# Loading the first tile in two pieces: the largest absolute value of each row, 8192 x 8192

## The chip, the cores and the metric

The kernel runs on one core of a Trainium2 chip. The metric is device time in microseconds (us) of one execution, the median of several; smaller is better. The core has several engines with queues of their own; this kernel uses VectorE (DVE) for all arithmetic, SyncE (SP) to issue nearly all transfers, ScalarE (ACT) for one store and GpSimd (POOL) for a few memory fills and the closing work. Sixteen DMA engines move the data.

## The reference

```
def setup_inputs():
    rows = 8192
    cols = 8192
    return {"x": np.random.randn(rows, cols).astype(np.float32)}

def reference(x):
    return np.linalg.norm(x, ord=np.inf, axis=1)
```

Along axis 1 of a matrix this norm is the largest absolute value of each row: 8192 rows of 8192 numbers give 8192 numbers. All 268.4 MB are read once; 32 KB are written.

## The kernel before

A tile is 128 partitions by 16384 columns of float32: each partition holds two neighbouring rows (B = 2), 64 KB that also lie together in memory. Three tiles have room at once (BUFS = 3). The 8192 rows are 32 such tiles, in three groups.

The bulk is 24 tiles, loops over `a` (A = 6) and `n` (G = 4). Each is one load of 8.4 MB by SP (L303) and one reduce by DVE, through the helper `absmax` (its instruction stands at L296), which takes the maximum of absolute values along the columns of both rows and writes two numbers per partition into `r_bulk`. The reduce of a tile waits for its load; the load of a tile waits for the reduce that last read its buffer, three tiles back. The first three loads wait for no reduce.

The next seven tiles, listed in `TAIL`, come in two to five loads by columns each (L315), with a reduce for each piece of a row into `part`. The last tile, `LAST`, comes in twelve loads (L341), from 2176 columns down to 768, so that little work is left when the last byte lands. Then SP stores `r_tail` (L359); ACT has stored `r_bulk` a little earlier (L357).

Loads rotate over eight completion semaphores. Where a load's semaphore is still in use, SP waits for the load eight places ahead.

After the program has been built, five functions edit it. Two matter here. `start_first_load_early` takes the first transfer that SP issues in the body, which must wait for nothing, and puts it at the very start of SP's program, ahead of the opening meeting of the engines (a barrier in which they wait for one another before the body begins). Exactly one transfer is moved; SP's next ones follow the meeting. `finish_on_pool` puts the waits for the last transfers and the clearing of semaphores on POOL at the end; it finds the last store's semaphore by itself.

The lines that the change touches are the load in the bulk's loop:

```
t = sbuf.tile([P, W + PAD], F32, tag="t")
nc.sync.dma_start(out=t[:, :W], in_=x_b[a, n])
```

W is 16384; PAD is 256 spare columns that the last tile uses.

Of the kernel before, what the change touches and what calls it, by code (L numbers as in the profile page):

```python
# [33 lines left out]


HEAD, STEP = 32, 8


def segments(loads, cols):

    out, at = [], 0
    for i, w in enumerate(loads):
        end = at + w
        while at < end:
            r = at // cols
            to = min(end, (r + 1) * cols)
            out.append((i, r, at - r * cols, to - at))
            at = to
    return out
# [201 lines left out]
@with_exitstack  # L251
def kernel(
    ctx: ExitStack,
    tc: tile.TileContext,
    x: bass.AP,
    out: bass.AP,
    G: int = 4,
    B: int = 2,
    BUFS: int = 3,
    PAD: int = 256,  # L260
    LINE: int = 128,
):
    nc = tc.nc
    P = nc.NUM_PARTITIONS
    rows, cols = x.shape
    W = B * cols


    n_tail = B * (len(TAIL) + 1)
    n_bulk_rows = rows // P - n_tail  # L270
    assert n_bulk_rows % (G * B) == 0
    A = n_bulk_rows // (G * B)
    split = n_bulk_rows * P
    x_b = x[:split].rearrange("(a p n b) c -> a n p (b c)", p=P, a=A, n=G, b=B)
    out_b = out[:split].rearrange("(a p n b) -> p a (n b)", p=P, a=A, n=G, b=B)
    x_t = x[split:].rearrange("(p t b) c -> t p (b c)", p=P, b=B)
    out_t = out[split:].rearrange("(p t) -> p t", p=P)

    outp = ctx.enter_context(tc.tile_pool(name="outp", bufs=1))
    sbuf = ctx.enter_context(tc.tile_pool(name="sbuf", bufs=BUFS))  # L280

    segs = [segments(loads, cols) for loads in TAIL]
    k_max = max(sum(r == b for _, r, _, _ in s) for s in segs for b in range(B))
    parts_of = [sum(r == b for r, _ in LAST) - 1 for b in range(B)]
    assert sum(parts_of) <= PAD

    r_bulk = outp.tile([P, A, G * B], F32)
    r_tail = outp.tile([P, n_tail], F32)
    part = outp.tile([P, n_tail - B, k_max], F32)
    used = [HEAD, A * G * B, n_tail, (n_tail - B) * k_max]  # L290
    gap = -sum(-(-n // STEP) * STEP for n in used) % LINE
    outp.tile([P, gap], F32, name="gap")
    nc.gpsimd.memset(part[:], 0.0)  # L293

    def absmax(o, i):
        return nc.vector.reduce_max(  # L296
            out=o, in_=i, axis=X, apply_absolute_value=True
        )

    for a in range(A):  # L300
        for n in range(G):
            t = sbuf.tile([P, W + PAD], F32, tag="t")
            nc.sync.dma_start(out=t[:, :W], in_=x_b[a, n])  # L303
            absmax(
                r_bulk[:, a, n * B : (n + 1) * B],
                t[:, :W].rearrange("p (b c) -> p b c", b=B),
            )

    for i, loads in enumerate(TAIL):
        t = sbuf.tile([P, W + PAD], F32, tag="t")  # L310
        todo = segs[i]
        seen = [0] * B
        at = 0
        for j, w in enumerate(loads):
            nc.sync.dma_start(out=t[:, at : at + w], in_=x_t[i][:, at : at + w])  # L315
            at += w
            for _, b, c, n in [s for s in todo if s[0] == j]:
                k, lo = seen[b], b * cols + c
                absmax(part[:, i * B + b, k : k + 1], t[:, lo : lo + n])
                seen[b] += 1  # L320

    def after(ins, first, kind):
        info = mybir.DependencyInfo(kind, mybir.DependencyReason.SCHED_ONLY)
        tc.add_manual_dep(ins.ins, first.ins.name, info, reason="order")


    t = sbuf.tile([P, W + PAD], F32, tag="t")
    left = parts_of[:]
    col = [0] * B
    at, slot = 0, {}  # L330
    ends = [w for _, w in LAST[-B:]]
    lo = W - sum(ends)
    for b in range(B):
        slot[b] = -(-lo // LINE) * LINE + ends[b]
        lo = slot[b] + parts_of[b]
    assert lo <= W + PAD
    for j, (b, w) in enumerate(LAST):
        final = left[b] == 0
        to = slot[b] - w if final else at
        frm = b * cols + col[b]  # L340
        nc.sync.dma_start(out=t[:, to : to + w], in_=x_t[len(TAIL)][:, frm : frm + w])  # L341
        col[b] += w
        if final:
            r = n_tail - B + b
            absmax(r_tail[:, r : r + 1], t[:, to : slot[b] + parts_of[b]])
        else:
            left[b] -= 1
            k = slot[b] + left[b]
            done = absmax(t[:, k : k + 1], t[:, to : to + w])
            at += w  # L350
        if j == 0:

            ins = absmax(r_tail[:, : n_tail - B], part[:])
            after(ins, done, mybir.DependencyClass.NoSync)
        if j == len(LAST) - 4:

            ins = nc.scalar.dma_start(out=out_b, in_=r_bulk[:])  # L357
            after(ins, done, mybir.DependencyClass.Sync)
    nc.sync.dma_start(out=out_t, in_=r_tail[:])  # L359
    nc.at_finalize(clear_partials_early)  # L360
    nc.at_finalize(drop_implied_waits)
    nc.at_finalize(start_first_load_early)
    nc.at_finalize(finish_on_pool)
    nc.at_finalize(open_without_vector)
# [30 lines left out]
```

## Time and profile before

| what | value |
|---|---|
| time, median of 3 runs | 626.8 us (626.56 to 627.16) |
| time of the profiled execution | 626.44 us |
| its span, first to last instruction | 623.8 us |
| read from memory | 268.44 MB, 430 GB/s over the span |
| DVE | 63 instructions, 552.4 us busy |
| bulk reduces | 24, 17.22 us each |
| loads of bulk tiles | 24, median 40.7 us from issue to landing |

The profile is one execution, taken by the hardware profiler; durations below come from it. A load's time to landing contains the time that it queues behind earlier loads: with a tile's data taking about 19.4 us (the distance between two landings in the bulk), 40.7 us means that one whole tile was ahead of it. A transfer moves as packets; a packet here is one partition's contiguous piece, and each of the sixteen DMA engines carries the packets of eight partitions. The trace records every packet with its start, duration and size. "Idle before" is time in which an engine had nothing to run, with what ended it.

### The profile page before, as it was taken

Reading aid. Unit: us, or ns where it says so; the run is one execution under the profiler, and the core shown is the slowest. Engines: PE = TensorE matmul, PEld = TensorE weight load, DVE = VectorE, ACT = ScalarE, POOL = GpSimd, SP = SyncE. Lnnn points to the kernel's source line nnn. Section 1 sums busy time; section 2 is a strip of 40 time slices with the busy share of each in tenths; the row PEclk is TensorE's granted clock in tenths of the full one; section 3 lists DMA queues with packets and bytes.
Section 4 is the critical chain, followed back from the end, with each engine's and each line's share of the span. In section 5 each row is a group of like instructions: output and inputs, shape, how many; then the busy total and the mean of one; then the engine's idle time right before and its main releaser. Section 6 shows DMA issues by size and latency. Waiting matters only on the chain.

```text
span 623.8 us, 151 instructions
## 1 busy us (share of the span) xinstructions
DVE 552.4 (89%) x63; POOL 0.3 (0%) x5
## 2 busy tenths in 40 slices
DVE  0588988889988899888898888988889999999999
POOL 0000000000000000000000000000000000000000
DMA  9999999999999999999999999999999999999998
GB/s 403 471 403 454 420 433 441 403 471 403 471 403 462 412 454 420 437 437 403 471 403 471 403 471 403 454 420 450 424 434 406 432 448 422 431 435 432 426 426 350
DMA packets 8849, 268.47 MB, mean 430 GB/s; under 512 B 1680, under 2 KB 1680, under 8 KB 3088
## 3 DMA queue, kind: packets, MB, share of 16 engines
q1 hardware_dynamic: 8064, 268.44, 99.7%
q10 hardware_dynamic: 784, 0.02, 0.1%
q14 instruction: 1, 0.01, 0.0%
HBM read 268.44 MB, written 0.03 MB: 430 GB/s over the span
## 4 chain that ended last, share of the span: by engine, by line
DMA 63%; DVE 36%; another core or an unknown queue 0%; issue 0%
DMA t<-in_x_dram 63%; DVE r_bulk L296 25%; DVE part L296 8%; DVE t L296 3%; DVE r_tail L296 0%
## 5 line engine op out<-in xcount | busy, mean ns | idle before, releaser
L296 DVE TENSOR_REDUCE r_bulk<-t 128x2 f32<-128x16384 f32 x24 | 413.3, 17220 | 70.4 <-DMA t<-in_x_dram 70.4
L296 DVE TENSOR_REDUCE part<-t 128x1 f32<-128x8192 f32 (+19 forms) x26 | 121.3, 4737 | 0.3
L296 DVE TENSOR_REDUCE t<-t 128x1 f32<-128x1792 f32 (+7 forms) x10 | 16.3, 1689 | 0.0
L296 DVE TENSOR_REDUCE r_tail<-t 128x1 f32<-128x772 f32 (+1 forms) x2 | 1.8, 952 | 0.0
L296 DVE TENSOR_REDUCE r_tail<-part 128x14 f32<-128x42 f32 x1 | 0.2, 184 | 0.0
L293 POOL MEMSET part<- 128x42 f32 x1 | 0.1, 133 | 0.0
L379 POOL MEMSET const-bfloat16-1.0<- 128x1 bf16 x1 | 0.1, 101 | 0.0
L379 POOL MEMSET const-uint8-127<- 128x1 uint8 x1 | 0.1, 101 | 0.0
L379 POOL MEMSET const-float32-0.0<- 128x1 f32 x1 | 0.1, 98 | 0.2 <-issue 0.2
L379 POOL MEMSET const-float32-1.0<- 128x1 f32 x1 | 0.1, 98 | 0.0
## 6 DMA issues: line engine op xcount, KB each, us to landing
t<-in_x_dram SPq DMA_DIRECT2D x2, 4672.0 KB, 37.5
t<-in_x_dram SPq DMA_DIRECT2D x2, 3520.0 KB, 36.2
t<-in_x_dram SPq DMA_DIRECT2D x1, 6336.0 KB, 36.3
t<-in_x_dram SPq DMA_DIRECT2D x1, 5696.0 KB, 40.4
t<-in_x_dram SPq DMA_DIRECT2D x2, 1792.0 KB, 34.3
t<-in_x_dram SPq DMA_DIRECT2D x1, 3392.0 KB, 37.6
t<-in_x_dram SPq DMA_DIRECT2D x1, 3008.0 KB, 44.2
t<-in_x_dram SPq DMA_DIRECT2D x1, 2496.0 KB, 27.3
```

Of the source, the lines that this page charges most:

```text
L293: nc.gpsimd.memset(part[:], 0.0)
L296: return nc.vector.reduce_max(out=o, in_=i, axis=X, apply_absolute_value=True)
L379: nc = _bacc.Bacc("TRN2", target_bir_lowering=False, num_devices=1)
```

## The change

In the bulk's loop, the first tile's load (a = n = 0) is cut at column 1024: one load of columns 0 to 1023 (512 KB, 4,096 bytes a partition) and one of columns 1024 to 16383 (7.5 MB, 61,440 bytes a partition). All other tiles are loaded as before. The first reduce still reads the whole tile.

```
@@ -34,6 +34,9 @@
 HEAD, STEP = 32, 8
+
+
+FIRST = 1024
@@ -300,7 +303,9 @@
     for a in range(A):
         for n in range(G):
             t = sbuf.tile([P, W + PAD], F32, tag="t")
-            nc.sync.dma_start(out=t[:, :W], in_=x_b[a, n])
+            cuts = [0, FIRST, W] if a == n == 0 else [0, W]
+            for lo, hi in zip(cuts, cuts[1:]):
+                nc.sync.dma_start(out=t[:, lo:hi], in_=x_b[a, n][:, lo:hi])
             absmax(
                 r_bulk[:, a, n * B : (n + 1) * B],
                 t[:, :W].rearrange("p (b c) -> p b c", b=B),
```

In the built program SP now issues 58 transfers instead of 57. The one that `start_first_load_early` moves ahead of the opening meeting is the load of 1024 columns; the load of 15360 columns is SP's first after it. The first reduce waits for two semaphores. Every later load uses the next of the eight semaphores, and the lists of the other engines are otherwise the same.

More of the change, by code (lines that the diff above doesn't have):

```diff
@@ L36 @@
 HEAD, STEP = 32, 8
+FIRST = 1024
 def segments(loads, cols):
@@ L302 @@
             t = sbuf.tile([P, W + PAD], F32, tag="t")
-            nc.sync.dma_start(out=t[:, :W], in_=x_b[a, n])
+            cuts = [0, FIRST, W] if a == n == 0 else [0, W]
+            for lo, hi in zip(cuts, cuts[1:]):
+                nc.sync.dma_start(out=t[:, lo:hi], in_=x_b[a, n][:, lo:hi])
             absmax(
```

## The prediction

> **What bounds the kernel now.** I read the page first (who is busy, what the end hangs on), then the rates of three long stretches, the chain of waits, and last the first six microseconds, where the edit acts.
>
> ```profile
> DVE 552.4 (89%) x63; POOL 0.3 (0%) x5
> DMA  9999999999999999999999999999999999999998
> DMA 63%; DVE 36%; another core or an unknown queue 0%; issue 0%
> L296 DVE TENSOR_REDUCE r_bulk<-t 128x2 f32<-128x16384 f32 x24 | 413.3, 17220 | 70.4 <-DMA t<-in_x_dram 70.4
> ```
>
> The DMA engines are full in nearly every one of the 40 slices. VectorE (DVE) is 89% busy and its only real idle time, 70.4 us, is spent waiting for loads of bulk tiles.
>
> ```profile
> core 0: us, DVE busy (x) POOL busy (x), PEclk, DMA share, GB/s
> 8.00:466.00 458.00, 396.05 (x23) 0.00 (x0) 1.00 1.00 434
> 466.00:600.00 134.00, 133.33 (x26) 0.00 (x0) 1.00 1.00 429
> 600.00:620.00 20.00, 20.00 (x12) 0.00 (x0) 1.00 1.01 422
> ```
>
> The last column is the rate. It holds 434 GB/s through the whole bulk, and falls a little in the tail, where loads are narrower and packets shorter. So the stream of loads has no hole that a better order could fill.
>
> ```profile
> 0.73 0.07 issue
> 0.79 40.36 DMA t<-in_x_dram
> 41.16 0.02 issue
> 41.18 17.22 DVE r_bulk L296
> ...
> 466.41 17.22 DVE r_bulk L296
> 483.63 17.26 DVE part L296 x3
> ```
>
> The columns are start, duration, and what held the chain. It runs from the second load's issue at 0.79 through landings and reduces. From 466.41 to the end DVE never idles noticeably: the reduce that starts there waited for the last bulk tile, and all that follows is DVE work or loads of the tail. A stream that is late by some amount in its first microseconds therefore ends late by that amount; one that is early gains it.
>
> ```profile
> 0.00 0.36 SPq L303 DMA_DIRECT2D t<-in_x_dram  x1
> 0.79 0.33 SPq L303 DMA_DIRECT2D t<-in_x_dram  x1
> DMA  0000009999900000000000009990909000000000
> 21.88 17.22 DVE L296 TENSOR_REDUCE r_bulk<-t 128x2 f32<-128x16384 f32 x1 [21.88 <-DMA t<-in_x_dram]
> 41.18 17.22 DVE L296 TENSOR_REDUCE r_bulk<-t 128x2 f32<-128x16384 f32 x1 [2.08 <-DMA t<-in_x_dram]
> ```
>
> SP issues the first load at 0.00 and the second, behind the opening meeting of the engines, at 0.79. The third line covers 0 to 6 us in slices of 0.15 and marks where packets start: sixteen between 0.99 and 1.55, one for each DMA engine, and the next sixteen from 3.73 on. The packet records give the sizes: a full load is 128 packets of 65,536 bytes, eight for each engine. The first sixteen took 2.74 to 3.23 us, nearly all later ones 2.418. The difference, 0.32 to 0.81 us, is a start-up cost paid once.
>
> **The change, part by part.** The 8.4 MB load that SP issues ahead of everything becomes one of 0.52 MB (128 packets of 4,096 bytes); the rest (128 packets of 61,440 bytes) is issued behind the opening meeting, where the load of the second tile stood. No other instruction is added or removed.
>
> *Packets.* In the tail, a load 1024 columns wide exists: its 128 packets took 159 ns each. A packet of 61,440 bytes has no row; between the rows for 50,688 bytes (1,872 ns) and 65,536 (2,418), a straight line gives 1,872 + 546 x 10,752 / 14,848 = 2,267 ns. Together 2,426 against 2,418: 8 ns a partition, eight partitions an engine, 0.067 us. Its bounds are 0.03 (the 422 of the last stretch against 434, for 0.52 MB: 1.242 against 1.208 us) and 0.13 (twice the worked value). On the path, since the stream has no slack.
>
> *Completion.* One more load is one more four-byte packet on each engine, 9 ns in the records. On the path: 0.009 us.
>
> *The hole that may open.* Until now 19 us of data covered the 0.79 us to the second issue. Now 0.52 MB must. On one engine that data lasts, from its first packet, 0.32 of start-up plus 8 x 159 ns = 1.59 us. If issue to first packet takes the second load what it took the first (0.99 to 1.55, by engine; ScalarE's late store took 0.92, from 620.33 to 621.25), the second's packets are ready 0.79 us after the first's on the same engine. The margin is 1.59 - 0.79 = 0.80 us. I take zero, hidden by the first load's own data; without that cover each further microsecond costs one. The third issue before took 0.70 us instead of 0.33, as if the issue path were briefly full; were that 0.37 to fall on the second half, 0.43 of margin remains.
>
> *Start-up.* How short packets behave on sixteen cold engines no row shows. The lower bound: every engine pays only the smallest excess; the last starter would be at 1.55 + 2.42 + 0.32 = 4.29 where the slowest first packet now ends at 4.62, so -0.33 us. The upper: the largest excess is paid again by the long packets, +0.81. I take 0, because the first load still starts at the same point and meets the same 0.32 to 0.81.
>
> *Waits and queues.* The first reduce now waits for two loads. Late in the trace, a DVE semaphore wait in front of a reduce takes 0.07 us (622.00 to 622.08). Behind it queues the second reduce, which idles 2.08 us for its own load, so it is hidden; uncovered it would cost 0.07. SP issues each load one place later: the loads of the second and third tile leave SP some 0.4 and 0.7 us later, with about 19 and 38 us of data ahead of them. Uncovered, that would cost those amounts. Loads rotate over eight completion semaphores, so each later load changes semaphore, but a tail load that waits for the one eight places ahead still waits for the same data. ScalarE's store shifts likewise. Zero.
>
> The sum is 0.067 + 0.009, about +0.08 us. The profiled execution took 626.44 us, 623.8 of span and 2.64 around it, so 626.52. The median shown is 626.8, 0.36 above the profiled run; measured as that was, 626.9.
>
> **A rule that speaks against it.** The Trainium skill, page "DMA: Bandwidth & Descriptors", section "Anatomy of one DMA", fits about 2.0 us fixed per DMA plus bytes over 436 GB/s, for GpSimd's path; its "Rules for kernel authors" ask for at least 1 MiB a load. Charged in full, the extra load of half that size would make the sum 628.9. The trace disagrees for queued loads: the tail's loads of 0.4 to 1.1 MB run at 422 GB/s, so the fixed part overlaps with the neighbour. It would return if the queue ran dry between the two.
>
> **The rivals.** *The stream runs dry (slower).* The second half comes after the first has drained. For: only 0.80 us of cover, and one trace's opening. Against: the waits listed for the built program show none between the halves but the opening meeting. Price, with the second half held until the first has landed: landing follows the last packet by 0.33 us in the first tile, then 1.55 to the same last engine's packet, then another start-up of 0.32 to 0.81: 2.2 to 2.7 us, about 629.2. It shows beyond 0.2% when the second issue comes later than 0.79 + 0.80 + 1.25 = 2.84 us after the first. 18% for this or another loss above 1.25 us.
>
> *A better start (faster).* Short packets get all engines going at once. Evenly warm engines give -0.33 + 0.08, so 626.55, which is no measurable change; to exceed 0.2% nearly all of 0.99 + 0.81 = 1.80 us before full flow would have to vanish, for 625.0 at best. 12%, since the cold start is the one thing the trace can't show with short packets.
>
> *The gain that a smaller first piece suggests is hidden anyway.* Reducing while the rest arrives would need a reduce of the piece alone; here one reduce waits for both. Even an earlier first reduce would only lengthen DVE's idle time before the second, 2.08 us now. It gives 626.9 too and belongs to the forecast.
>
> **How the numbers follow.** Forecast, no change: 70%; runs dry or some other loss: 18%; better start: 12%. Within 0.2% (1.25 us, about what a measurement of this kernel can tell from no change) means 625.55 to 628.05; the unknown costs alone span 626.8 - 0.33 + 0.04 = 626.5 to 626.8 + 0.81 + 0.14 = 627.75. With part of either rival, the range is 625.6 to 628.6.
>
> **What would show it.** Right: second issue near 0.79; 4,096-byte packets of about 159 ns after the first; long packets following on each engine without a gap; first reduce within 21.5 to 22.8; 434 GB/s in the bulk. Wrong: a blank stretch after the first sixteen groups of short packets, short packets far above 159 ns, a first reduce beyond 23.1 (21.88 + 1.25) or before 20.6, or a bulk rate off 434, since 1% there is over 4 us.

## The result, and the profile after

The changed kernel takes 627.62 us (median of 21 runs, 626.56 to 629.06) against 626.64 us (21 runs, 626.43 to 627.35): a ratio of 1.0016, interval 1.001 to 1.0022. That is 0.98 us slower, inside the band of 0.2% that the forecast called no change, and yet more than its interval. The runs lie nearly three times as wide as before's (2.50 us against 0.92), so part of the loss differs from one execution to the next.

Two rows of the changed kernel's page, who is busy and the bulk reduces:

```profile
DVE 552.5 (88%) x63; POOL 0.3 (0%) x5
L299 DVE TENSOR_REDUCE r_bulk<-t 128x2 f32<-128x16384 f32 x24 | 413.3, 17220 | 71.2 <-DMA t<-in_x_dram 71.2
```

DVE's work is unchanged, and it waited 0.8 us longer for bulk tiles (71.2 against 70.4). The rate over the first of the three stretches:

```profile
8.00:466.00 458.00, 396.05 (x23) 0.00 (x0) 1.00 1.00 432
```

The bulk ran at 432 GB/s instead of 434. Now the reduces of the early tiles, changed kernel first, then before. The bracket holds DVE's idle time ahead of each reduce.

```profile
21.97 17.22 DVE L299 TENSOR_REDUCE r_bulk<-t 128x2 f32<-128x16384 f32 x1 [21.97 <-DMA t<-in_x_dram]
41.24 17.22 DVE L299 TENSOR_REDUCE r_bulk<-t 128x2 f32<-128x16384 f32 x1 [2.05 <-DMA t<-in_x_dram]
...
99.66 17.22 DVE L299 TENSOR_REDUCE r_bulk<-t 128x2 f32<-128x16384 f32 x1 [2.29 <-DMA t<-in_x_dram]
119.13 17.22 DVE L299 TENSOR_REDUCE r_bulk<-t 128x2 f32<-128x16384 f32 x1 [2.25 <-DMA t<-in_x_dram]
138.68 17.22 DVE L299 TENSOR_REDUCE r_bulk<-t 128x2 f32<-128x16384 f32 x1 [2.33 <-DMA t<-in_x_dram]
...
177.37 17.22 DVE L299 TENSOR_REDUCE r_bulk<-t 128x2 f32<-128x16384 f32 x1 [2.05 <-DMA t<-in_x_dram]
```

```profile
99.24 17.22 DVE L296 TENSOR_REDUCE r_bulk<-t 128x2 f32<-128x16384 f32 x1 [2.11 <-DMA t<-in_x_dram]
118.55 17.22 DVE L296 TENSOR_REDUCE r_bulk<-t 128x2 f32<-128x16384 f32 x1 [2.09 <-DMA t<-in_x_dram]
137.89 17.22 DVE L296 TENSOR_REDUCE r_bulk<-t 128x2 f32<-128x16384 f32 x1 [2.12 <-DMA t<-in_x_dram]
...
176.59 17.22 DVE L296 TENSOR_REDUCE r_bulk<-t 128x2 f32<-128x16384 f32 x1 [2.10 <-DMA t<-in_x_dram]
```

The first two tiles arrive almost as before (21.97 against 21.88, 41.24 against 41.18). Then each load comes a little too late: in the rows shown DVE idles 2.25 to 2.33 us where before it idles 2.09 to 2.12. At 177.37 it is over, the loss stands at 0.78 us and grows by 0.03 more to the last bulk reduce (467.22 against 466.41).

The rest was lost at the very end. The chain of waits, before:

```profile
607.52 13.51 DVE t L296 x9
621.03 0.18 issue
621.21 0.81 DVE r_tail L296
```

and of the changed kernel, with one row of its list of waits:

```profile
608.35 13.75 DVE t L299 x9
622.10 0.28 issue
622.37 0.47 DVE r_tail L299
```

```profile
DVE r_tail L299 <- DVE t L299: 0.3, 1, 0.3
```

Consecutive reduces overlap: each starts about 0.08 us before the one ahead ends. The second last one, the first into `r_tail`, did so before (621.21, with the reduce ahead ending at 621.29). Now it starts 0.29 us after that end, though the load that it waits for had landed at 621.86, half a microsecond before that start, and DVE had passed its wait for it at 621.89. So the profiled spans differ by 0.09 (first reduce) + 0.72 (bulk) + 0.36 (tail) - 0.01 = 1.16 us, which is 624.96 - 623.80.

### The profile page after: what moved, and what is told of

It is laid out like the page before. It is cut to its first block, busy times and chain, and to the rows that moved or that the text cites. A ratio compares the mean times of both kernels' runs of the same rounds, so it can differ in the third digit from the quotient of the medians.

```text
span 625.0 us, 153 instructions
## 1 busy us (share of the span) xinstructions
DVE 552.5 (88%) x63; POOL 0.3 (0%) x5
## 4 chain that ended last, share of the span: by engine, by line
DMA 63%; DVE 36%; another core or an unknown queue 0%; DVEq 0%; issue 0%; SPq 0%
DMA t<-in_x_dram 63%; DVE r_bulk L299 25%; DVE part L299 8%; DVE t L299 3%; DVEq L395 0%; DVE r_tail L299 0%; SPq L308 0%
## 5 line engine op out<-in xcount | busy, mean ns | idle before, releaser
L299 DVE TENSOR_REDUCE r_bulk<-t 128x2 f32<-128x16384 f32 x24 | 413.3, 17220 | 71.2 <-DMA t<-in_x_dram 71.2
```

The source lines that it names most:

```text
L299: return nc.vector.reduce_max(out=o, in_=i, axis=X, apply_absolute_value=True)
```

## The experiments

Theory A: the cut itself is cheap, but starting sixteen engines on short packets leaves them in a pattern in which they slow one another until it settles. Theory B: the loss is that of any cut. Theory C: the stall at the end comes from the later loads having moved by one completion semaphore. D and E came up on the way. For each trace I read three numbers: the start of the first bulk reduce, the distance from first to last bulk reduce, and the gap in front of the second last reduce. The medians are set against before's runs taken beside them. Medians of 11 runs have an interval of about 0.0009 either way in the ratio, 0.55 us, so smaller differences of medians carry little alone, and the readings rest on the traces.

| kernel | runs | median over before, us | first reduce | first to last bulk reduce | gap at the end |
|---|---|---|---|---|---|
| before | | 0 | 21.88 | 444.53 | -0.08 |
| changed, 1024 first | 21 | +0.98 | 21.97 | 445.25 | +0.29 |
| the same again | 11 | +0.51 | 22.21 | 445.15 | +0.24 |
| 15360 first, then 1024 | 11 | +0.30 | 22.19 | 444.37 | +0.28 |
| thirteenth tile cut | 11 | +0.42 | 22.03 | 444.49 | +0.29 |
| halves | 11 | +0.47 | 21.91 | 445.07 | +0.27 |
| whole, one tiny load more | 11 | -0.06 | 22.06 | 444.46 | -0.08 |
| 1024 first, two tiny loads more | 11 | +1.32 | 23.21 | 444.38 | +0.24 |
| whole, one DVE instruction more | 11 | +0.27 | 21.98 | 444.48 | +0.22 |
| 15360 first, one DVE instruction more | 11 | +0.32 | 22.07 | 444.41 | -0.08 |
| 2048 first | 11 | +0.66 | 21.89 | 444.98 | +0.30 |
| 256 first | 11 | +1.54 | 22.67 | 444.96 | +0.27 |

### The wide piece first

```
-            cuts = [0, FIRST, W] if a == n == 0 else [0, W]
+            cuts = [0, W - FIRST, W] if a == n == 0 else [0, W]
```

> The first tile is still cut in two, but the early load is the wide piece (15360 columns) and the 1024 columns follow. Theory A (start-up): the cost of the change is not the second load but that the sixteen DMA engines start on short packets, leave the start in an uneven pattern, and slow one another in the next tiles until the pattern settles. Then this kernel starts as before's did: distance from the first bulk reduce to the last about 444.5 us (444.53 before, 445.25 in the changed kernel), time within 0.3 us of before. Theory B (the cut itself: one more load, odd packet lengths): as slow as the changed kernel, about 1.0 us over before.

Measured: 626.91 us against 626.61, all 11 runs within 0.25 us. The distance over the bulk is 444.37, none lost; the first reduce comes 0.31 us later, of which 0.16 is made up there. The 0.30 is about the gap at the end, which this kernel has too. Theory B falls for the bulk, and the gap is not a matter of the early piece.

### Another tile cut

```
+            cuts = [0, FIRST, W] if (a, n) == (3, 0) else [0, W]
```

> The thirteenth tile instead of the first is cut into 1024 and 15360 columns; the first tile is one load. Theory A: all engines are under way and settled by then, every stream is lengthened alike by 8 short packets, so +0.08 us, at most 0.3. Theory B: about 1.0 us over before, and the reduces after the thirteenth tile later by that much.

Measured: 627.03 us, +0.42, more than theory A allowed. The trace says why: nothing was lost in the bulk (444.49 us from first to last reduce, before 444.53), and the gap at the end is there. The last bulk reduce starts 0.11 us later than before's (466.52 against 466.41), but the first was 0.15 late already, twelve tiles ahead of the cut, and with nothing cut (one tiny load more, below) the last one starts at 466.52 too. So what a cut among running streams costs, 0.08 by the lengths of its packets, is too little to be seen here, and something that every cut brings costs 0.36 at the end.

### Two halves

```
-FIRST = 1024
+FIRST = 8192
```

> The first tile in two halves of 8192 columns, so the early load has packets of 32,768 bytes. Theory A: a start on long packets is a start like before's: +0.1 us, at most 0.4, distance first to last bulk reduce below 444.8. Theory B: about 1.0 us over before, as any cut.

Measured: 627.08 us, +0.47, of which 0.36 is the gap. But the profiled execution (627.34) lost 0.55 us in the bulk, in two steps of 0.3 behind the sixth and the eighth tile. Theory A had put the bound at 444.8, so in the form "long packets start well" it is wrong: a start on packets of 32,768 bytes can lose as well.

### The changed kernel again

> The changed kernel once more, for a second trace and for the spread. Theory A: first bulk reduce again near 21.97, then tiles further apart than 19.32 us until some tile, after which all distances are 19.32; where that ends, and so the loss, differs from the first trace (0.73 us there). Median about 1.0 us over before with a spread above before's 0.9 us. Theory B: the same loss at the same place. Theory C (the end): the 0.29 us by which the second last reduce came late in the first trace comes again, as something that the shifted semaphores cause; under A it comes or not by chance.

Measured: +0.51 us, 626.49 to 627.72. Counted against the settled 19.32 us a tile, the second trace loses 0.85 us behind the second, third and fourth tile (idle times of 2.38 and 2.57 us there) and nothing later; the first reduce is at 22.21. The place and the size of the loss are not fixed, the gap at the end is. This is what theory A said of the bulk, and it leaves theory C for the end.

### Semaphores moved, nothing cut

```
+    spare = outp.tile([P, 8], F32, name="spare")
...
+            if a == 0 and n == 1:
+                for k in range(0, 8, 8):
+                    nc.sync.dma_start(out=spare[:, k : k + 8], in_=x_b[a, n][:, k : k + 8])
```

> The kernel before, its first tile whole, with one extra load of 8 columns (4 KB in all, into a buffer that nothing reads) issued after the second tile's load: every later load moves on by one completion semaphore, as in the changed kernel, and the cut is gone. Theory C (semaphores): the second last load now signals the semaphore that shows a lag of 0.35 us from its last packet instead of 0.31, the second last reduce is told too late and starts about 0.28 us after the one before it ends, as in all five traces with a cut, instead of 0.08 before that. Time +0.4 to +0.5 us over before (0.36 of it the stall, up to 0.1 for the load). Theory A alone: no stall, at most +0.15 us.

Measured: 626.56 us, as before, and no gap. Its chain of waits:

```profile
607.66 13.55 DVE t L297 x9
621.21 0.10 issue
621.31 0.84 DVE r_tail L297
```

Theory C is refuted: the semaphores are moved as in the changed kernel, and the second last reduce follows on without a stall. The tiny load cost nothing that could be seen.

### Cut, and semaphores moved by three

The changed kernel with two such tiny loads.

> The changed kernel (1024 and 15360 columns) plus two extra loads of 8 columns each, so that later loads are moved by three semaphores and the second last load has one of short lag again. Theory C: the stall in front of the second last reduce is gone (start 0.08 us before the end of the reduce ahead), the time falls by 0.36 less what two tiny loads cost (up to 0.2). Theory A: the distances in the early tiles above 19.32 us stay, 0 to 1.5 us by chance. If the stall came from the extra wait on VectorE or from the cut, it stays here.

Measured: the gap stayed (0.24 us), a second blow to theory C. The time, 627.94 us, went up, and the first reduce started only at 23.21. The packets' starts between 2.9 and 4.1 us, in slices of 0.03 us, for the changed kernel and for this one:

```profile
DMA  0900000000000000000000000000000000000000
```

```profile
DMA  0009000000009000000000009000000000000900
```

In the changed kernel's trace the last engine passes from its short packets to its first long one at 2.94 and nothing starts after that, since all are busy; between their short and long packets the sixteen waited 0.1 us in all. Here all short packets have ended by 2.90, yet four engines start their first long packet only at 3.01, 3.26, 3.64 and 4.01. (An expectation below speaks of six; they are four.) They had run dry, the last one for at least 1.1 us. That is theory E: the second piece, issued at 0.80 in both kernels, does not reach every engine in time. The changed kernel's second trace has it on one engine: fifteen of the sixteen first long packets start within 0.01 us of the end of a short stream, and the sixteenth at 3.10, about 0.36 us after the one stream that is left over. The two tiny loads were issued after the second piece, but it is not shown that they had no part in this.

### Three cold starts, long packets and short

```
+            if (a, n) in ((2, 0), (4, 0)):
+                order(load, last)
-            absmax(
+            last = absmax(
```

`order` makes the load wait for the reduce just ahead, so the engines run dry; the second kernel cuts the three tiles at 1024 as well.

> The kernel before, but the loads of the ninth and the seventeenth tile wait until the reduce just ahead has ended, so that the DMA engines run dry twice and start again on packets of 65,536 bytes. It gives three cold starts in one run, for comparison with the next kernel; about 40 us longer than before by the two holes. Theory A: after each start the distances between reduces add up to little above 19.32 us each, as in the trace of before (0.2 us over seven distances).

> The same two holes, with the first, ninth and seventeenth tile cut into 1024 and 15360 columns, so that each of the three starts is on packets of 4,096 bytes; the second last load has a semaphore of short lag. Theory A: each start loses another 0.3 to 0.7 us on average in the tiles behind it, so the median stands 1 to 2 us above the kernel with long packets, and the distances behind the restarts add up to more. Theory B' (a cut costs its 0.08 us and what the changed kernel lost beside was chance or the end's stall): 0.25 us above.

Measured: 666.88 us (5 runs) and 667.74 (4 runs), +0.86, between the two expectations. But in the two traces, whose spans differ by 0.82 us, most of it arose after the bulk: the last bulk reduces differ by 0.18 us (506.98 against 506.80), and another 0.65 came in the tail, nearly all in one wait. In the lists of waits, long packets first:

```profile
DVE part L296 <- DMA t<-in_x_dram: 0.2, 1, 0.2
DVE part L299 <- DMA t<-in_x_dram: 1.0, 2, 0.8
```

What delayed that load stands under the next heading. Three starts on short packets, with their three cuts, cost 0.18 us in these traces and not theory A's 1 to 2. Long packets, around the first restart:

```profile
196.48 17.22 DVE L296 TENSOR_REDUCE r_bulk<-t 128x2 f32<-128x16384 f32 x1 [21.98 <-DMA t<-in_x_dram]
215.78 17.22 DVE L296 TENSOR_REDUCE r_bulk<-t 128x2 f32<-128x16384 f32 x1 [2.08 <-DMA t<-in_x_dram]
235.10 17.22 DVE L296 TENSOR_REDUCE r_bulk<-t 128x2 f32<-128x16384 f32 x1 [2.11 <-DMA t<-in_x_dram]
254.50 17.22 DVE L296 TENSOR_REDUCE r_bulk<-t 128x2 f32<-128x16384 f32 x1 [2.17 <-DMA t<-in_x_dram]
```

Short packets:

```profile
196.06 17.22 DVE L299 TENSOR_REDUCE r_bulk<-t 128x2 f32<-128x16384 f32 x1 [21.70 <-DMA t<-in_x_dram]
215.59 17.22 DVE L299 TENSOR_REDUCE r_bulk<-t 128x2 f32<-128x16384 f32 x1 [2.31 <-DMA t<-in_x_dram]
235.12 17.22 DVE L299 TENSOR_REDUCE r_bulk<-t 128x2 f32<-128x16384 f32 x1 [2.31 <-DMA t<-in_x_dram]
254.74 17.22 DVE L299 TENSOR_REDUCE r_bulk<-t 128x2 f32<-128x16384 f32 x1 [2.40 <-DMA t<-in_x_dram]
```

With the short piece the first tile behind the hole comes 0.28 us sooner (21.70 against 21.98; 0.45 at the second hole), and the next three each come 0.20 to 0.23 us later. Over seven distances it loses 0.72 and 0.96 us, against 0.18 and 0.47 with long packets. So at these restarts the short packets mostly moved the loss: sooner in the first tile, paid in those behind it, with 0.26 and 0.05 us more in the sum, of which 0.08 each is the cut's own packets. At this kernel's own start neither lost anything in the tiles behind it, so one start says little.

### Place in VectorE's program

The wait for two loads is one more instruction for DVE. In the built programs the second last reduce is, counting the branch that opens DVE's part, instruction 64 before and with the tiny load alone, 65 in every kernel with one cut, and 67 in the restarts with three, where no stall was seen. (DVE's own records in the traces give the same steps, each one lower without the branch.) Theory D: place 65 stalls. Edit of before, and then of the kernel with the wide piece first:

```
+            if a == 0 and n == 1:
+                absmax(spare[:, :1], t[:, :8])
```

> The kernel before with one extra VectorE instruction, a reduce of 8 columns of the second tile into a number that nothing reads, in a place where VectorE waits for loads anyway. No cut, no extra load. Theory D (place in VectorE's program): the second last reduce is now the 65th instruction that VectorE is given, as in every kernel with one cut, where it was the 64th in the kernel before and in the one with the extra load alone; it starts about 0.28 us after the reduce ahead ends, and the time is 0.35 us over before. If the stall belongs to the cut or to the wait for two loads: same as before within 0.1 us.

> The cut with the wide piece early (0.3 us over before, median 626.91, all within 0.25 us) plus the same extra VectorE instruction, so that the second last reduce moves on to place 66. Theory D: no stall (start 0.08 us before the end of the reduce ahead), 0.25 to 0.36 us less than without the extra instruction, so within 0.1 us of before: the cut itself then costs the +0.08 of the packets. Otherwise as slow as the wide-piece-first kernel, 0.3 over before.

Measured, before with one instruction more: 626.82 us, +0.27, lowest run 626.74 where before's lowest is 626.40. Its timeline:

```profile
620.27 1.07 DVE L297 TENSOR_REDUCE t<-t 128x1 f32<-128x896 f32 x1
621.57 1.82 DVE L297 TENSOR_REDUCE r_tail<-t 128x1 f32<-128x772 f32 x2 [0.22 <-DVE t L297]
```

The stall is there with nothing cut. And the wide piece first, with the same instruction, at place 66:

```profile
620.50 1.07 DVE L300 TENSOR_REDUCE t<-t 128x1 f32<-128x896 f32 x1
621.49 1.81 DVE L300 TENSOR_REDUCE r_tail<-t 128x1 f32<-128x772 f32 x2
```

The stall is gone. All nine traces with the reduce in place 65 have it (0.22 to 0.30 us), all five at 64, 66 or 67 do not. The time of the last kernel did not follow: 626.87 us, +0.32, as without the extra instruction, with runs that spread over 0.9 us. Its trace shows what came in place of the stall, and that of the restarts at place 67 shows the same. Each of the fourteen traces has, inside the span, one packet of 8,192 bytes on a queue named instruction; here it is in the kernel at place 66, in the 0.6 us from 591.7:

```profile
q14 instruction: 1, 0.01, 3.2%
```

In the twelve traces at place 64 or 65 it starts in the last 2 us of the span (622.21 before, 623.05 in the changed kernel), when every load has landed. At place 66 and 67 it starts at 591.81 and 627.53, among the loads of the tail. It takes 309 ns, and the data packet that starts as it ends takes 1,007 ns where its like take 479 (1,062 for 535 in the restarts), so one engine of the sixteen falls 0.84 us behind. In the restarts the load that DVE waits for next has landed from fifteen engines by 628.12 and from the last at 628.88: that is the wait of 0.8 us above. At place 66 the last engine is 0.30 us behind the rest at 595.95, and the tail takes 0.2 us longer than before's. What sends this packet, and why it comes earlier in these two kernels, was not tried.

So what makes the stall come and go is shown, the place; why place 65 stalls is not. That the cut is free without the stall is not shown either, since the kernel without it lost time to the instruction packet.

### A wider and a narrower early piece

> The changed kernel with 2048 columns instead of 1024 in the early piece: 1.2 us more of data cover the second issue. Theory E (some engines run dry between the pieces; in one trace of a 1024-column start six long packets began 0.1 to 1.1 us after the last short one had ended): no engine runs dry, no run above 628.2 us, median 0.4 to 0.7 over before (0.36 of it the stall at the end). Theory A alone (short packets leave an uneven start): spread and median stay as with 1024, 0.5 to 1.3 over before, some runs above 628.2.

> 256 columns in the early piece: eight packets of 1,024 bytes an engine last about 0.4 us, 0.9 us less than with 1024 columns. Theory E: the engines run dry in every run, first reduce 0.5 to 1.5 us later than with 1024 columns, median 1 to 2 us over before. Theory A alone: less short-packet time at the start, so no worse than the changed kernel, 0.5 to 1.0 over before.

Measured: with 2048 columns 627.21 us, +0.66, highest run 627.56. With 256 columns 628.09, +1.54, lowest run 627.52, first reduce at 22.67. Both are as theory E had them. But the median with 2048 lies in theory A's range too, and its trace, in which no engine runs dry, still loses 0.45 us in the bulk, so dry engines are not the whole of the loss. With 256 the packet records show it directly: the sixteen short streams end between 1.36 and 1.87 us, the first long packets start between 1.76 and 2.94 us. Runs above 628.2 us occur with 1024 first in part of the runs (5 of 21 of the changed kernel, none of the 11 of the same again, 2 of the 11 with two tiny loads), with 2048 and with halves in none of 22. Since the same kernel had 5 such runs in one set and none in another, their absence with 2048 says little. Engines that run dry by chance fit as a part of the changed kernel's spread, and its second trace, of the slowest run of that set (627.72), has one; no trace is of a run above 628.2, so it is not shown for them.

## Why the prediction was right

Right: the time, 627.62 in 625.6 to 628.6, and the forecast of no change by the 0.2% bound. The sum did less well than the band: it forecast +0.08 us, and 0.98 was measured. That the 0.9 us it missed stayed inside 0.2% is luck as far as the sum goes, for it put 0.36 of it at zero and had for the rest only a bound. By its steps:

- *Packets and completion, +0.08.* The short packets took 159 ns (median; 45 of the 128 more, up to 675), the long ones 2,267, as worked out. Right in the lengths; the effect on the time is too small to be seen (444.49 us over the bulk with a cut in the running stream, 444.53 before). The Trainium skill's fit of about 2.0 us fixed per DMA ("DMA: Bandwidth & Descriptors", "Anatomy of one DMA") is for GpSimd's path. A load that SP queues behind another did not pay it here: the cut of the thirteenth tile added nothing to the bulk, and the measurement decides.
- *The hole, zero with 0.80 us of margin.* Right in the changed kernel's first trace, where the engines waited 0.1 us in all. The margin was taken from one start and as the same for every engine. In the second trace one engine waited 0.36 us, and with two tiny loads more four did, one for at least 1.1 us. So the rival "the stream runs dry" is real on single engines in some executions, and not through a late issue (0.80 in all of these).
- *Start-up, taken as 0 between -0.33 and +0.81.* The larger of the two wrong sizes. In the traces of starts on 1024 columns the first reduce and the bulk together stood 0.81 us (changed kernel), 0.96 (again) and 1.18 (two tiny loads) above before's, and 0.13 below it after eight tiles at the start of the kernel with restarts. The gain was seen at the restarts, 0.28 and 0.45 us in the first tile, with a loss behind it. That the first trace's 0.81 equals the upper bound is chance: I looked for the loss inside the first packets, and in the changed kernel's two traces most of it came tiles later.
- *Waits and queues, "Zero".* Wrong, by 0.36 us. "No other instruction is added or removed" left out that DVE's wait for the second load is one. The wait itself was hidden where it stands, as said. What it displaced was not priced: every later DVE instruction moves on one place, and one of them stalls there.
- *The bulk rate.* A rate off 434 was named as what would show the forecast wrong, "1% there is over 4 us". It came, as 432, but the loss was about 0.4% over the first nine tiles alone, 0.7 us, and the forecast held.

Of the change's 0.98 us, 0.36 are the stall and 0.08, worked out, the packets. The rest, 0.5 us in the median and -0.5 to +2 in single runs against before's median, is found by subtraction and put down to the start, where both traces of the kernel have their other loss. In the second set of runs (+0.51) it is under 0.1. Why the engines take longer after such a start stays open.

## What to carry to other kernels

In a kernel that is bound by transfers from the first byte to the last, an edit at the start is paid at the end one for one, and a piece meant to cover a later issue must cover the slowest of sixteen engines, not the issue time. When an edit adds even a hidden instruction, compare the places of the last instructions on that engine: the end lost 0.36 us to one place here, and two kernels a place or two further on lost 0.2 and 0.65 behind an instruction packet among their loads. Where runs of one kernel spread much wider than another's, take several traces before explaining one.

## What the runs showed of the hardware

- Engines that do not run out of packets can still take longer over one: of the packets of 65,536 bytes behind the start, 158 took over 2.425 us in before's trace (up to 2.51) and 367 in the changed kernel's (up to 2.56), none over 2.44 later than 194 us, by when the distance of tiles had settled at 19.32 us. In the settled state the spacing in which the engines finish a tile repeated to a few nanoseconds over the last ten bulk tiles of both kernels (spread 0.66 us before, 0.81 in the changed kernel). That the engines slow one another is an inference; what the packets contend for was not tried.
- The first packet starts about 0.99 us after the issue, the last engine's between 1.55 and 2.0 in the eight traces that start on packets of 32,768 bytes or more. The Trainium skill gives about 0.6 us to the first byte for this path ("DMA: Bandwidth & Descriptors", "Latency and other measured facts"); no run here showed less than 0.98.
- The second last reduce at place 65 of VectorE's program starts 0.22 to 0.30 us after the reduce ahead ends, at 64, 66 and 67 0.08 to 0.10 us before it. Whether instructions come to the engine in blocks of 64 was not tried.
- A packet of 8,192 bytes on the instruction queue that falls among queued loads costs its engine more than its own 309 ns: the next data packet took 1,007 ns instead of 479, and 1,062 instead of 535 (one case each).
